# Block 1's keys, queries and output gates by seven products of block sums, and two of four forward state products in other PSUM banks

## The chip, the cores and the metric

The kernel runs on one core of one Trainium2 chip. The metric is the device time of one execution in microseconds (us). Five engines work side by side, each on its own queue in order: PE (TensorE, matrix products into PSUM), DVE (VectorE), ACT (ScalarE), POOL (GpSimd) and SP (SyncE, which only issues DMAs here). PSUM has eight banks; one 128x512 float32 tile fills one.

## The reference, cut to what matters

```
h = x + mlstm_mixer(rmsnorm(x), ...)          # S = 2048 tokens, D = 1024
  u = xn @ w_in                               # q, k: 512 columns each; v, o: 1024 each; 16 gates
  h_fwd = mlstm_scan(q, k, v, i, f); h_bwd = the same on the flipped sequence
     # per chunk of 128 tokens: num = (s*d) v + inter * q C;  C = decay*C + (w*v) k^T
  h = norm(h_fwd + h_bwd) * head_norm * sigmoid(o);  mix = h @ w_out
h = h + sqrelu_mlp(rmsnorm(h), w1, w2)        # D_FF = 4096
h = h + sigmoid(rmsnorm(h) @ gate_w + b) * (p @ ple_w);  out = rmsnorm(h)
```

The change touches the first product, `xn @ w_in`, for the upper half of the tokens, and the update of the forward state `C`.

## The kernel before

Every float32 product is three products of rounded parts: an operand is cut into a high part (cast to fp32r on ACT) and the rest (subtraction on DVE) by `split`, and `mm3` (L161) adds high*high, high*rest and rest*high in PSUM.

The tokens are two blocks of 1024. Block 1 comes first: its values and gates (tiles `psv`, two jobs of `v_jobs`), then 4 slabs of 128 key features, 4 of queries and 8 of output gates. A slab is a `slab_job`: for each 512 tokens `feat_group` runs 8 blocks of the contraction times 3 matmuls of 128x128 by 128x512 into one bank (`psf`), and ACT or DVE moves the result to an `ev` tile, which goes to DRAM (`kq_d`, `og_d`; keys also transposed to `kt_d`). `run` walks over the jobs: the weights of the next are split while the groups of the present one run. Steps woven in between prepare block 0's tokens (`Early`: load `raw`, squares on ACT into `junk`, scaling and 32x32 transposes on DVE, store to `mix_d`).

Block 0 follows in the same way, with the backward scan woven in; then the forward scan over 16 chunks. In a chunk PE does, in this order (table `ORDER`): `n0`, the forward numerators (4 tiles `pn`, one for each head); `s`, the state update (4 tiles `pu`, L100 by `state_update`, moved out on DVE as `Cn`); `T`, eight transposes into two tiles `pth`; `S`, the scores of the next chunk (`pS`); `n1`, the backward numerators (4 `pn`); `o0 o1`, the output product (2 `pso`). ACT moves `pn` out as `nt`.

PSUM is dealt out by tag: `ps_mm` has four banks (`pn`, `pso`, `psf`, `psv`, and before the change all forward `pu`), `ps_tr` has three (`pth`, `ptg`, `pt`), `ps_s` one (`pS`). A new tile of a tag takes a bank whose last tile has been read; PE waits for that. SBUF tiles are dealt out likewise: tag `H` has 39 slots of 4 KB a partition, `O` 7, `S` 6.

The MLP after the scan already works by seven products: a product of 2x2 blocks is made of 7 products of sums of blocks in place of 8 (`SEVEN`, `products`, `Left` for the weights' sums, `Job7`, `run7`). The seven accumulate in three banks; each bank is read out between its products, and the parts are added on DVE. Nearly all instructions are recorded on a helper's line, L100, so tiles tell them apart.

Of the kernel before, what the change touches and what calls it, by code (L numbers as in the profile page):

```python
# [16 lines left out]
P = 128  # L17
# [18 lines left out]
def hybrid_mlstm_kernel(  # L36
# [153 lines left out]
    class Weight:  # L190
# [3 lines left out]
            self.srcs = src if isinstance(src, list) else [src]  # L194
            self.shape = shape

        def dma(self):
            self.st = Ht("wst", self.shape)
# [158 lines left out]
    class Early(Prep):  # L357
# [20 lines left out]
                self.raw = None  # L378

        def get(self, m):  # L380
            self.z[m] = shuffled(self.d, m)

        def tr(self, k):
            t = Ht("xT", [P, 2, 512], F32R)
# [17 lines left out]
    wcol = const.tile([P, P], F32, name="wcol")  # L402
    ecol = const.tile([P, P], F32, name="ecol")
    dcb = const.tile([P, P], F32, name="dcb")


    gt = {}
# [14 lines left out]
    def store(c, dst, src):  # L422
        (SP if c >= 8 else G).dma_start(dst, src)
# [237 lines left out]
    def bwd_steps(c):  # L661
        s = {}

        def load():
            s["kt"] = kt_load(c, Ot)
            s["v"] = v_load(c)

        def one():
            s["vx"] = v_split(s["v"], m=V)
            s["wk"] = wk_of(s["kt"], 1, c)  # L670

        def two():
# [5 lines left out]
        return [load, one, two]  # L678


    wo = [rows_w(w_out, k * P) for k in range(KD)]
# [1 line left out]
    class Chunk:  # L683
# [130 lines left out]
        def out(self, n):  # L814
# [5 lines left out]
            if n == 1:  # L820
# [1 line left out]

    NF = DFF // P
    NQ = S // 256
    SEVEN = [("A11", "B11", 0), ("A12", "B21", 2), ("S2", "T2", 0), ("S1", "T1", 1), ("S3", "T3", 0),
             ("S4", "B22", 1), ("A22", "T4", 0)]  # L830
    sub_, add_ = ALU.subtract, ALU.add
# [7 lines left out]
    def products(A_, B_, n, after):  # L839
        ps = [None] * 3  # L840

        def product(i, an, bn, bk):
            def f():
                first = ps[bk] is None
                if first:
                    ps[bk] = (ps_mm, ps_mm, ps_tr)[bk]("p" + "abc"[bk])
                for k in range(n):
                    ah, al = A_.get(an, k)
                    bh, bl = B_.get(bn, k)
                    mm3(ps[bk], ah, al, bh, bl, first and k == 0, k == n - 1, skip_group_check=not first)  # L850
                after(i, ps[bk])
            return f
        return [product(i, *s) for i, s in enumerate(SEVEN)]

    def hi_lo(shape):

        n = 1
        for s in shape[1:]:
            n *= s
        if n <= 512:  # L860
            t = Ht("op", [P, 2] + list(shape[1:]), F32R)
            return t[:, 0], t[:, 1]
        return Ht("op", shape, F32R), Ht("op", shape, F32R)

    class Left:


        def __init__(self, n):
            self.n, self.ops = n, {}

        def preps(self, eng, eng2=None):
            n, eng2 = self.n, eng2 or eng

            def alloc():
                if n > 2:
                    self.s = [Ht("sa", [P, 2, n, P]) for _ in range(2)]
                else:
                    t = Ht("sa", [P, 4, n, P])
                    self.s = [t[:, 0:2], t[:, 2:4]]

            def s12():
                alloc()
                (r1, r2), s = self.r, self.s[0]
                eng.tensor_tensor(s[:, 0], r1[:, :, P:], r2[:, :, P:], op=add_)  # L884
                eng.tensor_tensor(s[:, 1], s[:, 0], r1[:, :, :P], op=sub_)

            def s34():
                (r1, r2), s = self.r, self.s
                eng2.tensor_tensor(s[1][:, 0], r1[:, :, :P], r1[:, :, P:], op=sub_)
                eng2.tensor_tensor(s[1][:, 1], r2[:, :, :P], s[0][:, 1], op=sub_)  # L890

            def op(names, src, cut):
                def f():
                    t = src()
                    hl = hi_lo(t.shape)
                    split(hl[0], hl[1], t)
                    for i, nm in enumerate(names):
                        self.ops[nm] = lambda k, i=i: tuple(cut(x, i, k) for x in hl)
                return f
            by_col = lambda x, i, k: x[:, k, i * P:(i + 1) * P]  # L900
            by_row = lambda x, i, k: x[:, i, k]
            return [s12, op(["A11"], lambda: self.r[0][:, :, :P], by_col),
                    op(["A12", "A22"], lambda: self.r[1], by_col), s34,
                    op(["S1", "S2"], lambda: self.s[0], by_row),
                    op(["S3", "S4"], lambda: self.s[1], by_row)]

        def get(self, nm, k):
            return self.ops[nm](k)

    class Left1(Left):  # L910


        def __init__(self, f):
            super().__init__(4)
            self.f = f

        def dma(self):
            self.r = []
            for j in range(2):
                t = Ot("wst", [P, 4, 256])  # L920
                SP.dma_start(t, w1[j * 512:j * 512 + 512, self.f * 256:self.f * 256 + 256].rearrange("(k p) n -> p k n", p=P))
                self.r.append(t)

    class Left2(Left):

# [58 lines left out]

        def get(self, nm, k):
            return self.pairs[k].ops[nm]

    class Right1:


        def __init__(self):
            self.z, self.ops = {}, {}

        def split(self, nm):
            for m in range(2):
                hl = hi_lo([P, 2, 512])
                split(hl[0], hl[1], self.z[nm, m])
                self.ops[nm, m] = hl

        def get(self, nm, k):  # L1000
            hi, lo = self.ops[nm, k // 2]
            return hi[:, k % 2], lo[:, k % 2]

    class Tokens0(Right1):

# [99 lines left out]
    class Job7:  # L1105
        def __init__(self, left, B_, n, after, prep=None):
            self.left, self.groups = left, products(left, B_, n, after)
            self.prep = left.preps(V) if prep is None else prep
            self.side, self.post = [], [[] for _ in self.groups]

    def run7(jobs):
        def dma(i):
            if i < len(jobs):
                jobs[i].left.dma()
        for i, j in enumerate(jobs):
            if i == 0:
                dma(1)
            dma(i + 2)
            nxt = jobs[i + 1].prep if i + 1 < len(jobs) else []

            def both(g, post):
                def f():
                    g()
                    for h in post:
                        h()
                return f
            weave([both(g, p_) for g, p_ in zip(j.groups, j.post)], nxt + j.side)

    def up_job(blk, B_, f):

# [156 lines left out]
    seq = []  # L1287
    for b in (1, 0):
        jobs[b, "v"] = v_jobs(pa[b], b)
        jobs[b, "k"] = [slab_job(pa[b], b, KC + h * P, kq_evac(0, h)) for h in range(H)]  # L1290
        jobs[b, "q"] = [slab_job(pa[b], b, QC + h * P, kq_evac(1, h), (ps_mm, (ps_tr, ps_mm)[b])) for h in range(H)]
        jobs[b, "o"] = [slab_job(pa[b], b, OC + j * P, o_evac(j)) for j in range(KD)]
# [46 lines left out]
    p0.tr1(3)  # L1339
    strict()  # L1340
    v0.groups = [lambda: weave(v0g[3:4], pa[1][1].steps()[2:])] + v0g[4:]
    jobs[1, "k"][0].side.append(lambda: gate_rows(1))
    jobs[1, "k"][1].side.append(gate_bias)

    for nm, pr in (("k", pa[0][0]), ("q", pa[0][1])):
        e = pr.early()
        for j, f in zip(jobs[1, nm], (e[0:1], e[1:2], e[2:4], e[4:6])):
            j.side += f
    o = jobs[1, "o"]
    o[5].side += pa[0][0].gets()  # L1350
    o[6].groups, o[7].groups = [o[6].groups[0], o[7].groups[0]], [o[6].groups[1], o[7].groups[1]]
    o[6].weights, o[7].weights = o[6].weights + o[7].weights, []
    o[7].side += pa[0][0].trs() + pa[0][1].gets()
# [196 lines left out]
```

## Time and profile before

| | |
|---|---|
| median of 3 runs | 2457.06 us (2454.72 to 2457.98) |
| profiled execution: time / span of its trace | 2456.72 / 2455.0 us |
| busy in the span: PE, DVE, ACT, POOL | 98%, 62%, 46%, 24% |
| block 1's keys, queries, gates | 117.9 to 296.1 us |
| forward scan, about | 604 to 957 us |

A busy matrix engine is no proof that it works at its peak: consecutive matmuls overlap in the profile, so the time that one costs is the distance between starts. The chunks and stages are told apart by the times at which their tiles appear.

### The profile page before, as it was taken

How to read it: one execution, taken by the hardware profiler on the slowest of the kernel's cores; microseconds unless marked ns; L12 is line 12 of the kernel's file. 1: busy time of each engine (PE TensorE's matmuls, PEld its weight loads, DVE VectorE, ACT ScalarE, POOL GpSimd, SP SyncE). 2: the span in 40 equal slices, each digit the busy share in tenths (PEclk: the TensorE clock that was granted, in tenths of full speed). 3: DMA queues.
4: the chain of work that ended last, by engine and by line, in shares of the span. 5: the costliest groups of instructions: out<-in, count | busy, mean ns of one | idle time of the engine just before them, and what ended most of it. 6: DMA issues, size and time to landing. Idle time of an engine off the chain costs nothing.

```text
span 2455.0 us, 31650 instructions
## 1 busy us (share of the span) xinstructions
PE 2402.5 (98%) x11413; PEld 1978.5 (81%) x11413; DVE 1514.4 (62%) x2533; ACT 1131.9 (46%) x2134; POOL 592.5 (24%) x609
## 2 busy tenths in 40 slices
PE   7999999999999999999999999999999999999998
PEld 6988898788888887888888888787887888887776
DVE  6152426556778888666674455766676667666665
ACT  5031414336777875343353333444443444445554
POOL 1030022124333333345633333011111111110000
PEclk9999999999999999999999999999999999999999
DMA  7178337868667775455763332567677776893211
GB/s 254 49 199 248 94 90 237 264 209 311 221 218 263 254 263 173 123 165 163 267 230 105 104 107 73 164 141 180 147 176 171 173 171 156 184 227 100 78 55 49
DMA packets 270133, 420.72 MB, mean 171 GB/s; under 512 B 46440, under 2 KB 181992, under 8 KB 269976
## 3 DMA queue, kind: packets, MB, share of 16 engines
q1 hardware_dynamic: 211416, 299.03, 37.3%
q0 software_dynamic: 58272, 119.15, 20.5%
q8 instruction: 89, 1.46, 0.2%
q14 instruction: 68, 0.56, 0.1%
q10 hardware_dynamic: 288, 0.52, 0.1%
HBM read 253.43 MB, written 165.01 MB: 170 GB/s over the span
## 4 chain that ended last, share of the span: by engine, by line
PE 54%; DVE 3%; ACT 1%; DMA 1%; issue 1%; SPq 0%; POOL 0%; ACTq 0%; DVEq 0%; POOLq 0%
PE pa L100 27%; PE pb L100 13%; PE pc L100 7%; PE pg L100 5%; PE pl L100 1%; DMA hst<-hid_d 1%; PE pt L100 1%; DVE h L100 1%; ACT L100 1%; DMA wst<-in_mlp_w 1%; DVE xs L100 1%; DVE op L100 1%; DVE rst L100 0%; DVE raw L100 0%; DVE g L100 0%
## 5 line engine op out<-in xcount | busy, mean ns | idle before, releaser
L100 PE MATMUL pa<-op 128*128 128x512 f32 x3072 | 754.2, 395 | 7.4 <-ACT e L100 4.3
L100 PEld LDWEIGHTS pa<-op 128*128 128x128 f32 x3072 | 575.4, 188 | 147.5 <-ACT e L100 7.2
L100 PE MATMUL pb<-op 128*128 128x512 f32 x1536 | 384.3, 394 | 0.9 <-DVE op L100 0.8
L100 PEld LDWEIGHTS pb<-op 128*128 128x128 f32 x1536 | 288.2, 188 | 70.0 <-DVE op L100 1.1
L100 PE MATMUL psf<-xT,whi 128*128 128x512 f32 x1024 | 322.0, 395 | 0.0
L100 DVE TENSOR_TENSOR op<-sa,op 128x768 fp32r<-128x768 f32 (+2 forms) x160 | 168.3, 1058 | 139.7 <-ACT op L100 106.8
L1162 POOL DMA_DIRECT2D h_d<-o x96 | 93.0, 976 | 563.3 <-DVE o L100 515.2
L100 PEld LDWEIGHTS psf<-xT,whi 128*128 128x128 f32 x1024 | 192.1, 189 | 43.9
L100 ACT COPY e<-pa 128x512 f32<-128x512 f32 x160 | 93.8, 586 | 259.4 <-PE pa L100 258.7
L100 ACT CAST op<-sa 128x768 fp32r<-128x768 f32 (+2 forms) x160 | 139.5, 879 | 147.8 <-PE pb L100 69.0
L100 PE MATMUL psf<-xT,wlo 128*128 128x512 f32 x512 | 202.2, 395 | 0.0
L100 PE MATMUL pc<-op 128*128 128x512 f32 x768 | 191.5, 394 | 0.2 <-DVE op L100 0.2
L100 PEld LDWEIGHTS pc<-op 128*128 128x128 f32 x768 | 144.1, 188 | 34.1 <-DVE op L100 0.6
L100 PE MATMUL psv<-whi,xT 128*128 128x272 f32 (+2 forms) x720 | 161.6, 318 | 0.6 <-DVE xT L98 0.6
L100 PEld LDWEIGHTS psv<-whi,xT 128*128 128x128 f32 x720 | 119.1, 189 | 9.9 <-DVE xT L98 0.8
L100 DVE TENSOR_TENSOR op<-wst,op 128x512 fp32r<-128x512 f32 x96 | 108.1, 1128 | 28.7 <-ACT op L100 16.1
L100 ACT CAST op<-wst 128x512 fp32r<-128x512 f32 x96 | 79.1, 834 | 95.1 <-DVE op L100 61.4
L884 POOL TENSOR_TENSOR sa<-wst 128x512 f32<-128x512 f32 x32 | 57.7, 1803 | 261.7 <-PE pb L100 158.2
L100 PEld LDWEIGHTS psf<-xT,wlo 128*128 128x128 f32 x512 | 96.6, 189 | 22.6
L100 PE MATMUL psv<-wlo,xT 128*128 128x272 f32 (+2 forms) x360 | 114.3, 317 | 0.0
L100 DVE TENSOR_TENSOR wlo<-wst,whi 128x1024 fp32r<-128x1024 f32 (+2 forms) x64 | 77.0, 1212 | 56.7 <-ACT whi L100 44.1
L100 PE MATMUL pso<-whi,hThi 128*128 128x512 f32 x256 | 102.4, 401 | 5.9 <-ACT nt L100 4.4
(228 smaller groups left out, 4257.5 us busy)
## 6 DMA issues: line engine op xcount, KB each, us to landing
wst<-in_mlp_w SPq DMA_DIRECT2D x96, 512.0 KB
h_d<-o POOLq DMA_DIRECT2D x96, 512.0 KB, 12.5
hid_d<-e SPq DMA_DIRECT2D x128, 256.0 KB
hst<-hid_d SPq DMA_DIRECT2D x64, 384.0 KB
wst<-in_mlstm_w_in SPq DMA_DIRECT2D x44, 512.0 KB
vst<-v_d SPq DMA_DIRECT2D x31, 512.0 KB
raw<-in_x SPq DMA_DIRECT2D x16, 512.0 KB
kq<-kq_d SPq DMA_DIRECT2D x16, 512.0 KB
```

The source lines that it names most:

```text
L100: r = f(*a, **kw)
L884: eng.tensor_tensor(s[:, 0], r1[:, :, P:], r2[:, :, P:], op=add_)
L1162: G.dma_start(rows(h1_d, 2 * q + i), o[i], accum_op=add_)
```

## The change

Two things. First, block 1's 16 slabs become 8 pairs of slabs. Of a pair the weights (1024x256) are 2x2 blocks of 512x128 and block 1's tokens (1024 features x 1024 tokens) 2x2 blocks of 512x512; the pair is made by the seven products, each of 4 blocks of the contraction times 3 matmuls. The sums of tokens `T1` to `T4` are made once on DVE while the values' second job runs, stored to DRAM (`ta_d`, by POOL's queue) and loaded again. The sums of weights are made for each pair on DVE. The transposed keys are stored by head pairs, in runs of 64 floats where there were 128. Second, in the forward scan the state products of heads 0 and 1 take `ps_tr` banks.

`products`, `hi_lo`, `Left`, `Right1`, `Job7` and `run7` are moved up in the file unchanged; `LeftW` is the old `Left1` for any weight and column. Steps that were hung on the slabs are hung on the pairs.

```diff
-            pu = (ps_tr if d == 1 and h % 2 else ps_mm)("pu")[:, :DVX]
+            pu = (ps_tr if (h % 2 if d == 1 else h < 2) else ps_mm)("pu")[:, :DVX]
...
+    class TokensA(Right1):
+        def parts(self, nm, k):
+            pr, k = self.prs[int(nm[2]) - 1], k + 4 * (int(nm[1]) - 1)
+            return pr.hi[k], pr.lo[k]
+        def get(self, nm, k):
+            return self.parts(nm, k) if nm[0] == "B" else super().get(nm, k)
...
+            return [t1, less("T2", "B22", "T1"), less("T3", "T2", "B11"), less("T4", "B21", "T2")]
...
+    def pair_job(B_, blk, col, finish, scale=None):
+        e = {}
+        def after(i, ps):
+            t = St("ev", [P, 512])
+            if i in (0, 2, 3, 6):
+                if scale is None:
+                    A.copy(t, ps)
+                else:
+                    A.activation(t, ps, AF.Copy, scale=scale)
+                if i < 6:
+                    e[i] = t
+                else:
+                    finish(t, 1, 0)
+            else:
+                t = e.pop({1: 0, 4: 3, 5: 2}[i])
+                if scale is None:
+                    V.tensor_tensor(t, ps, t, op=add_)
+                else:
+                    V.scalar_tensor_tensor(t, ps, scale, t, op0=ALU.mult, op1=add_)
+                finish(t, *{1: (0, 0), 4: (1, 1), 5: (0, 1)}[i])
+        left = LeftW(w_in, col)
+        return Job7(left, B_, 4, after)
...
-    seq = [j for nm in "vkqo" for j in jobs[1, nm]]
-    seq += [jobs[0, "v"][1], jobs[0, "v"][0]] + jobs[0, "k"] + o[:6] + [qa, fin]
+    pairs1 = kp + qp + op_
+    seq = [jobs[0, "v"][1], jobs[0, "v"][0]] + jobs[0, "k"] + o[:6] + [qa, fin]
...
+    for n, pr in ((0, pa[0][0]), (2, pa[0][1])):
         e = pr.early()
+        pairs1[n].side += e[0:2]
+        pairs1[n + 1].side += e[2:6]
...
+    mk = [xa.make(m) for m in range(2)]
+    vj.side += [f for i in range(4) for f in (mk[0][i], mk[1][i])]
+    vj.side += [f1.left.dma, lambda: xa.zload("T2"), lambda: xa.zload("T1")] + f1.prep[:3] + [lambda: xa.split("T2")] + f1.prep[3:] + [
+        lambda: xa.split("T1")]
+    f1.post[0] += [lambda: xa.zload("T3"), lambda: xa.zload("T4")]
...
+    run([v0, vj])
+    run7(pairs1)
+    jobs[0, "v"][1].ready = True
     run(seq)
```

PE's queue where the values of block 1 end and the keys begin. Before, the gates' transpose `ptg` and then the slabs:

```order
L100 MATMUL psv<-wlo,xT 128x256
L100 MATMUL psv<-whi,xT 128x256
L100 MATMUL ptg<-ident,gt 128x128
L100 MATMUL psf<-xT,whi 128x512 x2
L100 MATMUL psf<-xT,wlo 128x512
```

Now:

```order
L100 MATMUL psv<-wlo,xT 128x256
L100 MATMUL psv<-whi,xT 128x256
L100 MATMUL pa<-xT,op 128x512 x12
L100 MATMUL pc<-xT,op 128x512 x12
L100 MATMUL pa<-op 128x512 x12
L100 MATMUL pb<-op 128x512 x12
L100 MATMUL ptg<-ident,gt 128x128
L100 MATMUL pa<-op 128x512 x12
L100 MATMUL pb<-xT,op 128x512 x12
L100 MATMUL pa<-op 128x512 x12
```

The seven products of a pair stand one after the other, and `ptg` has moved behind the fourth.

ACT's queue from the fourth product of the first pair to the first of the second, now (`z` are the loaded token sums, `sa` the weights' sums, `op` the high and low parts, `junk` the squares of block 0's tokens):

```order
L100 ACTIVATE ev<-pb 128x512
L100 CAST op<-z 128x1024
L100 CAST op<-sa 128x1024 x2
L100 ACTIVATE junk,sse_1361<-raw 128x1024
L100 ACTIVATE ev<-pa 128x512
L100 ACTIVATE junk,sse_1361<-raw 128x1024 x2
L100 CAST op<-wst 128x512
L100 ACTIVATE junk,sse_1361<-raw 128x1024
L100 ACTIVATE ev<-pa 128x512
```

Casts and squares stand between two readings of a product's bank, where before they stood between readings of finished slabs.

PE's queue in a chunk of the forward scan (chunk 8) from the last state product on. Before:

```order
L100 MATMUL pu<-vh,wk 128x258
L100 MATMUL pth<-ident,jk 128x128 x8
L100 MATMUL pS<-kq 128x128 x4
L100 MATMUL pn<-vh,pTh 128x258
L100 MATMUL pn<-vl,pTh 128x258
```

Now:

```order
L100 MATMUL pu<-vh,wk 128x258
L100 MATMUL pth<-ident,jk 128x128 x4
L100 MATMUL pS<-kq 128x128
L100 MATMUL pth<-ident,jk 128x128 x4
L100 MATMUL pS<-kq 128x128 x3
L100 MATMUL pn<-vh,pTh 128x258
```

The second `pth` has moved behind a score product here and in chunks 1, 2 and 9; in the other chunks the order of PE is as it was. The orders of DVE and ACT in the scan are unchanged but for one step in chunk 1.

## Rows read from the trace of the kernel before

**Rows 1.** The page: busy times, the granted clock by slices, a costly group.

```profile
PE 2402.5 (98%) x11413; PEld 1978.5 (81%) x11413; DVE 1514.4 (62%) x2533; ACT 1131.9 (46%) x2134; POOL 592.5 (24%) x609
...
PEclk9999999999999999999999999999999999999999
...
L100 PE MATMUL psf<-xT,whi 128*128 128x512 f32 x1024 | 322.0, 395 | 0.0
```

**Rows 2.** Busy times by stretch: length, each engine, granted clock, DMA share, GB/s.

```profile
60.00:118.00 58.00, 58.00 (x435) 55.85 (x433) 6.35 (x18) 3.79 (x9) 0.00 (x0) 1.00 0.14 48
118.00:296.00 178.00, 178.00 (x770) 144.19 (x769) 66.47 (x121) 51.51 (x77) 28.18 (x48) 1.00 0.62 185
604.00:720.00 116.00, 110.14 (x660) 95.70 (x660) 90.38 (x183) 88.23 (x243) 44.53 (x56) 1.00 0.71 240
720.00:957.00 237.00, 227.46 (x1329) 197.67 (x1327) 205.41 (x393) 183.92 (x486) 76.35 (x89) 1.00 0.72 245
957.00:1340.00 383.00, 380.94 (x1637) 306.92 (x1638) 249.90 (x268) 152.15 (x216) 183.10 (x129) 1.00 0.54 173
```

**Rows 3.** Waits of PE, 604 to 940: us in total, times, longest.

```profile
PE pn L100 <- DVE Cn L100: 4.7, 6, 1.6
PE pso L100 <- ACT nt L100: 4.4, 6, 1.4
PE pu L100 <- ACT nt L100: 2.5, 6, 0.8
```

**Rows 4.** PE's timeline at both ends of block 1's slabs: start, length.

```profile
117.95 0.71 PE L100 MATMUL psf<-xT,whi 128*128 128x512 f32 x2
...
295.90 0.39 PE L100 MATMUL psf<-xT,wlo 128*128 128x512 f32 x1
296.13 0.28 PE L100 MATMUL psv<-whi,xT 128*128 128x272 f32 x1
```

**Rows 5.** Groups by shape on DVE and ACT in the MLP's stages: busy, mean ns.

```profile
L100 DVE TENSOR_TENSOR op<-wst,op 128x1024 fp32r<-128x1024 f32 x3 | 3.7, 1219 | 0.9 <-PE pa L100 0.9
...
L100 DVE TENSOR_TENSOR e<-pc,e 128x512 f32<-128x512 f32 x3 | 2.0, 683 | 1.6 <-PE pc L100 1.6
...
L100 ACT CAST op<-sa 128x1024 fp32r<-128x1024 f32 x31 | 32.5, 1050 | 58.5 <-PE pb L100 30.0 <-DVE op L100 14.8 <-issue 6.4
L100 ACT COPY e<-pa 128x512 f32<-128x512 f32 x30 | 17.5, 583 | 61.9 <-PE pa L100 61.9
```

**Rows 6.** Waits of PE in the MLP's first product, 957 to 1340.

```profile
PE pa L100 <- ACT e L100: 1.5, 1, 1.5
PE pa L100 <- DVE op L100: 0.7, 1, 0.7
PE pa L100 <- DVE e L100: 0.4, 2, 0.2
```

**Rows 7.** DMA issues: KB each, median us from issue to landing.

```profile
kt_d<-y POOLq DMA_DIRECT2D x16, 128.0 KB, 5.8
```

**Rows 8.** PE's timeline in chunk 13, and DVE's reading of the state products.

```profile
872.28 1.03 PE L100 MATMUL pth<-ident,jk 128*128 128x128 f32 x8
873.15 1.06 PE L100 MATMUL pS<-kq 128*128 128x128 f32 x8
873.97 0.36 PE L100 MATMUL pn<-vh,pTh 128*128 128x258 f32 x1
...
873.03 1.66 DVE L100 SCALAR_TENSOR_TENSOR Cn<-Cn,dcb,pu 128x258 f32<-128x258 f32 x4
```

**Rows 9.** The same in chunk 14, up to the output product.

```profile
893.61 1.03 PE L100 MATMUL pth<-ident,jk 128*128 128x128 f32 x8
896.65 0.39 PE L100 MATMUL pn<-vh,pTh 128*128 128x258 f32 x1 [1.11 <-DVE Cn L100]
...
901.18 0.51 PE L100 MATMUL pso<-whi,hThi 128*128 128x512 f32 x1 [0.49 <-ACT nt L100]
...
896.12 1.65 DVE L100 SCALAR_TENSOR_TENSOR Cn<-Cn,dcb,pu 128x258 f32<-128x258 f32 x4
```

More of the change, by code (lines that the diff above doesn't have):

```diff
@@ L404, in hybrid_mlstm_kernel, with products, product, f @@
     dcb = const.tile([P, P], F32, name="dcb")
+    NF = DFF // P
+    NQ = S // 256
+    SEVEN = [("A11", "B11", 0), ("A12", "B21", 2), ("S2", "T2", 0), ("S1", "T1", 1), ("S3", "T3", 0),
+             ("S4", "B22", 1), ("A22", "T4", 0)]
+    sub_, add_ = ALU.subtract, ALU.add
+    def products(A_, B_, n, after):
+        ps = [None] * 3
+        def product(i, an, bn, bk):
+            def f():
+                first = ps[bk] is None
+                if first:
+                    ps[bk] = (ps_mm, ps_mm, ps_tr)[bk]("p" + "abc"[bk])
+                for k in range(n):
+                    ah, al = A_.get(an, k)
+                    bh, bl = B_.get(bn, k)
+                    mm3(ps[bk], ah, al, bh, bl, first and k == 0, k == n - 1, skip_group_check=not first)
+                after(i, ps[bk])
+            return f
+        return [product(i, *s) for i, s in enumerate(SEVEN)]
@@ new lines, in hybrid_mlstm_kernel, with __init__, dma, split @@
+    class LeftW(Left):
+        def __init__(self, w, c0):
+            super().__init__(4)
+            self.w, self.c0 = w, c0
+        def dma(self):
+            self.r = []
+            for j in range(2):
+                t = Ot("wst", [P, 4, 256])
+                SP.dma_start(t, self.w[j * 512:j * 512 + 512, self.c0:self.c0 + 256].rearrange("(k p) n -> p k n", p=P))
+                self.r.append(t)
+    class Right1:
+        def __init__(self):
+            self.z, self.ops = {}, {}
+        def split(self, nm):
+            for m in range(2):
+                hl = hi_lo([P, 2, 512])
+                split(hl[0], hl[1], self.z[nm, m])
+                self.ops[nm, m] = hl
+        def get(self, nm, k):
+            hi, lo = self.ops[nm, k // 2]
+            return hi[:, k % 2], lo[:, k % 2]
@@ new lines, in hybrid_mlstm_kernel, with __init__, run7, dma @@
+    class Job7:
+        def __init__(self, left, B_, n, after, prep=None):
+            self.left, self.groups = left, products(left, B_, n, after)
+            self.prep = left.preps(V) if prep is None else prep
+            self.side, self.post = [], [[] for _ in self.groups]
+    def run7(jobs):
+        def dma(i):
+            if i < len(jobs):
+                jobs[i].left.dma()
+        for i, j in enumerate(jobs):
+            if i == 0:
+                dma(1)
+            dma(i + 2)
+            nxt = jobs[i + 1].prep if i + 1 < len(jobs) else []
+            def both(g, post):
+                def f():
+                    g()
+                    for h in post:
+                        h()
+                return f
+            weave([both(g, p_) for g, p_ in zip(j.groups, j.post)], nxt + j.side)
@@ L678, in bwd_steps, with __init__, get, make @@
         return [load, one, two]
+    ta_d = dram.tile([4, 2, P, 2, 512], F32, name="ta_d")
+    class TokensA(Right1):
+        def __init__(self, prs):
+            super().__init__()
+            self.prs = prs
+        def parts(self, nm, k):
+            pr, k = self.prs[int(nm[2]) - 1], k + 4 * (int(nm[1]) - 1)
+            return pr.hi[k], pr.lo[k]
+        def get(self, nm, k):
+            return self.parts(nm, k) if nm[0] == "B" else super().get(nm, k)
+        def make(self, m):
+            s = {}
+            def new(nm):
+                s[nm] = Ot("z", [P, 2, 512])
+            def store(nm):
+                G.dma_start(ta_d[int(nm[1]) - 1, m], s[nm])
+            def t1():
+                new("T1")
+                for i in range(2):
+                    t, (h2, l2), (h1, l1) = s["T1"][:, i], self.parts("B12", 2 * m + i), self.parts("B11", 2 * m + i)
+                    d = St("d", [P, 512])
+                    V.tensor_tensor(t, h2.bitcast(F32), h1.bitcast(F32), op=sub_)
+                    V.tensor_tensor(d, l2.bitcast(F32), l1.bitcast(F32), op=sub_)
+                    V.tensor_tensor(t, t, d, op=add_)
+                store("T1")
+            def less(nm, a, b):
+                def f():
+                    new(nm)
+                    for i in range(2):
+                        t = s[nm][:, i]
+                        if a[0] == "T":
+                            for n_, x_ in enumerate(self.parts(b, 2 * m + i)):
+                                V.tensor_tensor(t, s[a][:, i] if n_ == 0 else t, x_.bitcast(F32), op=sub_)
+                        else:
+                            h_, l_ = self.parts(a, 2 * m + i)
+                            V.tensor_tensor(t, h_.bitcast(F32), s[b][:, i], op=sub_)
+                            V.tensor_tensor(t, t, l_.bitcast(F32), op=add_)
+                    store(nm)
+                return f
+            return [t1, less("T2", "B22", "T1"), less("T3", "T2", "B11"), less("T4", "B21", "T2")]
+        def zload(self, nm):
+            for m in range(2):
+                self.z[nm, m] = Ot("z", [P, 2, 512])
+                SP.dma_start(self.z[nm, m], ta_d[int(nm[1]) - 1, m])
@@ new lines, in kq_pair, with finish @@
+    def kq_pair(B_, blk, qk, hp):
+        yy = {}
+        def finish(t, i, l):
+            h, c0 = 2 * hp + i, blk * 8 + 4 * l
+            t = t.rearrange("p (c t) -> p c t", c=4)
+            SP.dma_start(kq_d[c0:c0 + 4, :, qk, h, :].rearrange("c p t -> p c t"), t)
+            if qk:
+                return
+            if l not in yy:
+                yy[l] = [Ht("y", [P, 2, 8, 2, 32]), 0]
+            y = yy[l][0]
+            for m in range(2):
+                V.transpose(y[:, m, :, i, :], t[:, 2 * m:2 * m + 2].rearrange("p c (b i) -> p (c b) i", i=32))
+            yy[l][1] += 1
+            if yy[l][1] == 2:
+                for m in range(2):
+                    for a in range(4):
+                        G.dma_start(kt_d[(c0 + 2 * m) * P:(c0 + 2 * m + 2) * P, a, 64 * hp:64 * hp + 64].rearrange("(b i) e -> i b e", i=32),
+                                    y[32 * a:32 * a + 32, m].rearrange("i b h j -> i b (h j)"))
+        return pair_job(B_, blk, (QC if qk else KC) + hp * 256, finish, None if qk else DK ** -0.5)
@@ L681, in hybrid_mlstm_kernel, with o_pair, finish @@
+    def o_pair(B_, blk, jp):
+        def finish(t, i, l):
+            j, c0 = 2 * jp + i, blk * 8 + 4 * l
+            act(t, t, AF.Sigmoid)
+            V.tensor_scalar_mul(t, t, gains["hn"][:, j:j + 1])
+            SP.dma_start(og_d[c0:c0 + 4, :, j, :].rearrange("c p t -> p c t"), t.rearrange("p (c t) -> p c t", c=4))
+        return pair_job(B_, blk, OC + jp * 256, finish)
     wo = [rows_w(w_out, k * P) for k in range(KD)]
@@ L837, in hybrid_mlstm_kernel @@
     tz_d = dram.tile([4, 2, P, 2, 512], F32, name="tz_d")
[L839 to L908, printed above, removed]
@@ L910, in hybrid_mlstm_kernel @@
-    class Left1(Left):
-        def __init__(self, f):
[L914 to L922, printed above, removed]
+    class Left1(LeftW):
+        def __init__(self, f):
+            super().__init__(w1, f * 256)
@@ L986, in get @@
             return self.pairs[k].ops[nm]
[L988 to L1002, printed above, removed]
     class Tokens0(Right1):
@@ L1103, in zload @@
                     SP.dma_start(self.z[nm, m], tz_d[int(nm[1]) - 1, m])
[L1105 to L1127, printed above, removed]
     def up_job(blk, B_, f):
```

84 lines of the change are left out of this document (66 added, 18 removed).

## The prediction

> **What bounds the kernel now.** I read the page's busy times first, then stretches, then PE's waits. PE is busy 98% of the span at the upper of its two clock levels (2.4 GHz) nearly throughout [rows 1], so only two things can shorten the kernel: fewer or shorter matmuls, and less of the little time in which PE waits. The stretches say where that is. Block 1's slabs, 118 to 296 us, have PE busy 178 of 178 us, with DVE at 66 and ACT at 52 [rows 2]: there every matmul taken away is worth its full price, and DVE and ACT have room. The forward scan is another matter: from 604 to 957 PE is idle for 15 us while DVE is at 78 and 87% [rows 2], and PE's waits are for PSUM banks that DVE (`Cn`) or ACT (`nt`) has not yet read [rows 3].
>
> **The price of a matmul.** The group row gives 395 ns for one 128x512 matmul [rows 1], but that is from entry to end, and they overlap. The first of block 1's slab matmuls starts at 117.95, and the first one behind them at 296.13 [rows 4]. In between are 16 slabs x 2 halves x 8 x 3 = 768, so one costs 178.18 / 768 = 0.232 us. This is the price that I use; 0.395 would overstate the change by 70%. The Trainium skill, TensorE: Matmul & The Clock Gate, section Back-to-back issue gap, gives about 131 ns for matmuls of 512 columns in a sustained stream with their weight loads. By it the change would save 96 x 0.131 = 12.6 us; this stage itself shows 232, so the measurement decides and the figure gets no chance.
>
> **Removed.** A pair of slabs cost 96 matmuls, and costs 7 x 4 x 3 = 84 now. 8 pairs: 96 fewer, 96 x 0.232 = **22.3 us less**, at the same shapes and the same clock. The stage should take 672 x 0.232 = 155.9 us.
>
> **Added: the token sums.** T1 is made in 12 operations of 128x512 on DVE, T2 to T4 in 8 each, 36 in all. At 0.683 us (a 128x512 addition, rows 5) that is 24.6 us. With them come the first pair's 4 weight sums (2.7 us), its low parts (3.5 tiles of 1024 at 1.219, 4.3 us) and the low parts of T2 and T1 (4.9 us): 36.5 us of DVE. They stand beside the values' matmuls, 60 to 118 us, in which DVE works for 6 of 58 us [rows 2]. So they are hidden and I take nothing; without that cover they would cost all of 36.5. The DMAs that carry the sums out and back (8 MB) fall where the DMA engines are busy 14% of the time [rows 2]. T3 and T4 are fetched only in the first pair, but are wanted by its fifth and seventh product, 11.1 and 16.7 us after its start.
>
> **Added: read-outs between products.** A product is 12 matmuls, 2.78 us, a pair 84, 19.5 us. Its first, third, fifth and last product add into one bank, so ACT or DVE must have read that bank while the one product in between runs: 0.58 us of work (ACT's copy, rows 5) under a cover of 2.78. What can be late is the queue: casts of 1.05 us [rows 5], or the squares of block 0's tokens, stand before the read-out. In one pair DVE now does 4 sums, 3.5 low parts and 3 additions, 2.7 + 4.3 + 2.0 = 9.1 us; if all it did before in this stage stays (66 us / 8 = 8.3, an upper bound, since old splits and copies are in it) it is at 17.4 of 19.5. ACT does 3.5 casts and 4 copies, 6.0, at most 6.4 more from before: 12.4 of 19.5. Both fit, DVE without much to spare. A wait is below nothing in no case, since PE had none here. The nearest row is the MLP's first product, the same seven products: 383 us hold 2.6 us of such waits, 2.2 of them where the stage is entered [rows 6]. This stage has an entry too, so I take **2.4 us**; for the range 0 to 12 (the starved pairs below).
>
> **The two moved state products.** They were put where PE waits most: for the first `pn` of `n1` until DVE has read `pu` (4.7 us in 6 chunks), and for `pu` until ACT has read `pn` (2.5 us) [rows 3]. With heads 0 and 1 in `ps_tr` both waits lose their cause. But `ps_tr` has three banks: two `pu` and the first `pth` fill them, so the second `pth` must wait until DVE has read a `pu`. That wait is the old one in an earlier place. What it is worth stands in two chunks:
> - Chunk 13, no wait before: `pth` starts at 872.28, its second half 0.43 later at 872.71, scores at 873.15, `pn` at 873.97 [rows 8]. DVE starts on `Cn` at 873.03; chunk 14 shows PE going on 0.53 us after that start (896.12, 896.65) [rows 9]. The second `pth` could start at 873.56, so PE loses 0.85 us.
> - Chunk 14, a wait of 1.11 before: the second `pth` starts when `pn` did, at 896.65, and only then come its 0.44 us and the scores' 0.82, which used to run under the wait. `pn` is 1.26 later. Behind it `pso` waited 0.49 for ACT [rows 9], whose order hangs on DVE and not on PE, so that much is absorbed: 0.77 lost.
>
> I went through all chunks in the same way. 7 and 10 are like 13 (0.6, 0.5); 8, 11 and 12 like 14 (0.5, 0.7, 0.8; in 8 three of the four scores still come behind); in 9 the loss of 0.6 goes into a `pso` wait of 1.0; chunk 2 gains the 0.6 that `pu` waited for `nt`; in 1 and 4 what is gained goes into the next wait; in 3, 5 and 6 DVE is in time. Sum: 0.85 + 0.77 + 1.1 + 2.0 - 0.6 = **4.1 us more**. Its bounds are -7.2 (both waits vanish and nothing takes their place) and +10 (eight chunks at 1.26).
>
> **The sum.** The profiled execution took 2456.72 us (span 2455.0), 0.3 under the median of 2457.06. 2456.7 - 22.3 + 2.4 + 4.1 = **2441 us**.
>
> **Rivals.**
> - *The banks do help.* If DVE came to `Cn` before the second `pth` in chunks 7 to 14, as it does in 3, 5 and 6, the waits of 7.2 us would go, part of it into `pso`; I take 5. For it: DVE follows PE in some chunks, so that an earlier `pu` could pull `Cn` forward. Against it: in chunk 14 DVE starts `Cn` 2.5 us after `pth` began. 2456.7 - 22.3 + 2.4 - 5 = 2432 us.
> - *Starved pairs.* The low parts and token sums now hold 28 of 39 `H` slots (12 tiles of block 1's tokens, 16 of sums), and 11 are left for a pair's 7, the next pair's 9, and the transposes `y`. A `y` slot comes free when its DMA has landed, 5.8 us after issue for 128 KB [rows 7]. The key stores are now twice as many with runs of 256 bytes. If in four early pairs an operand waits for such a slot, PE loses 5.8 less a cover of 2.78, 12 us in all in place of 2.4: 2450.5 us. For it: POOL's queue carries both kinds of `y` in the first four pairs. Against it: products five and six need their operands late in a pair. The Trainium skill, DMA: Bandwidth & Descriptors, section Specifications, says that transfers under 512 bytes miss the line rate, as the DMA engine then reads, changes and writes back. That speaks against these stores; no row here shows runs of 256 bytes.
> - *Slower than before.* ACT reads the pairs' first bank late in every pair. The gain of 22.3 less 4.1 is used up at 18.2 / 8 = 2.3 us of waits in each pair. That needs read-outs that come 2.78 + 2.3 = 5.1 us after a product, five casts in a row before one copy. ACT's order has at most three casts or squares there. At 4 us a pair it would be 2456.7 - 22.3 + 4.1 + 32 = 2470 us.
> - *The price is another.* If the sevenfold products ran at another spacing than 0.232 the saving would scale; PE's clock is full in both stages [rows 2], and nothing speaks for it.
>
> **Chances.** Forecast 66%, with a range of its own of 2436 to 2447; banks help 17%; starved pairs 13%; slower 3%; another price 1%. The range of 2431 to 2450 holds the forecast, the case of the banks, and the milder half of the starved pairs. A measurement of this kernel can tell about 0.2%, 5 us, from no change. Faster by more than that (under 2452): 94%, the forecast, the banks and most of the starved pairs. Within it 4%, slower 2%.
>
> **What would show it.** Right: 672 matmuls `pa`, `pb`, `pc` in some 156 to 159 us; DVE near 40 us between 60 and 118, PE busy throughout; waits of PE in the pairs of 1 to 4 us, most in the first two; in the scan a new wait `pth <- DVE Cn` in chunks 7 to 14, `pn <- Cn` gone, `pso <- nt` smaller, and PE's idle time there larger than before. Wrong: the scan shorter (the banks help); waits of PE for `op` in pairs 1 to 4 with DVE waiting for a DMA of `kt_d` or `mix_d` (starved); waits of `pa` for ACT's `ev` in every pair (slower).

## The result and the profile after

The changed kernel takes **2441.27 us** (median of 4 runs, 2440.1 to 2444.73), the kernel before 2455.94 beside it (4 runs, 2454.72 to 2457.98). The ratio is 0.9942, 95% interval 0.9925 to 0.9959: 10 to 18 us faster. The forecast was 2441. The profiled execution took 2440.1 us with a span of 2438.4, 16.6 less than the span before.

The page of the changed kernel: busy time, granted clock by slices, the group that answers to `psf` [rows 1].

```profile
PE 2379.7 (98%) x11317; PEld 1962.4 (80%) x11317; DVE 1592.3 (65%) x2641; ACT 1168.6 (48%) x2182; POOL 606.3 (25%) x633
...
PEclk9999999999999999999999999999999999999999
...
L100 PE MATMUL pa<-op 128*128 128x512 f32 x3360 | 824.7, 394 | 7.7 <-ACT e L100 4.0
```

96 matmuls are gone (11413 to 11317); the mean of this group is 394 ns, that of `psf` was 395. The stretches that answer to [rows 2] (length, PE, PEld, DVE, ACT, POOL, granted clock, DMA share, GB/s):

```profile
60.00:116.00 56.00, 56.00 (x426) 54.20 (x425) 38.13 (x65) 12.03 (x18) 4.53 (x8) 1.00 0.66 228
116.00:273.00 157.00, 156.44 (x675) 126.22 (x675) 105.35 (x175) 73.72 (x111) 37.74 (x64) 1.00 0.71 215
579.00:695.00 116.00, 109.73 (x665) 96.50 (x664) 90.79 (x183) 88.82 (x244) 44.19 (x56) 0.99 0.71 241
695.00:941.00 246.00, 231.35 (x1322) 202.33 (x1320) 204.67 (x391) 186.22 (x485) 76.40 (x89) 0.97 0.69 236
941.00:1324.00 383.00, 380.75 (x1637) 307.18 (x1638) 252.36 (x269) 152.64 (x216) 182.67 (x129) 1.00 0.54 173
```

Three things are to be seen. DVE works 38 us ahead of the pairs, where it worked 6, and PE doesn't notice. The pairs keep PE busy for 156.4 of 157 us. And the scan's second stretch is 9 us longer than before, at a granted clock of 0.97 instead of 1.00. PE's timeline at both ends of the pairs, which answers to [rows 4] (start, length):

```profile
115.94 1.32 PE L100 MATMUL pa<-xT,op 128*128 128x512 f32 x5
...
270.11 2.96 PE L100 MATMUL pa<-op 128*128 128x512 f32 x12
272.92 0.29 PE L100 MATMUL psv<-whi,xT 128*128 128x272 f32 x1
```

From 115.94 to 272.92 are 156.98 us for 672 matmuls, against 178.18 for 768: **21.2 us less**. PE's waits in the changed kernel (us in total, times, longest), which answer to [rows 3]:

```profile
PE pth L100 <- DVE Cn L100: 14.6, 11, 3.0
...
PE pso L100 <- ACT nt L100: 3.5, 5, 2.0
...
PE pu L100 <- ACT nt L100: 0.7, 1, 0.7
...
PE pa L100 <- ACT ev L100: 0.6, 1, 0.6
```

The wait `pn <- Cn` is gone and `pth <- Cn` stands in its place, three times as large. The wait for `ev` is the only one in the pairs. Cutting both timelines at the same instructions (the stage's first product; the `psv` behind it; the `pu` of chunk 0; the MLP's first `pa`; the end of the span) shows where the 16.6 us come from:

| stretch | before | after | difference |
|---|---|---|---|
| up to block 1's keys | 117.95 | 115.94 | -2.0 |
| block 1's keys, queries, gates | 178.2 | 157.0 | -21.2 |
| up to the scan | 289.8 | 287.8 | -2.0 |
| scan, chunk 0's `pu` to the MLP | 343.2 | 352.6 | **+9.4** |
| MLP to the end | 1525.9 | 1525.0 | -0.9 |

The total agrees with the forecast, but not by the forecast's terms: the scan lost 9.4 us where 4.1 were expected, and 4.0 us came from two stretches in which no matmul was taken away.

**The granted clock.** Falls of the clock that happened in one execution and not in the other are more than enough for those 4.0 us. Between 462 and 474 us the kernel before had a granted clock of 0.72 (3.4 us lost), the changed one at the same place (438 to 450) 1.00. Between 36 and 48 us the window of the kernel before shows 0.86:

```profile
36.00:48.00 12.00, 10.46 (x48) 8.18 (x48) 7.69 (x14) 5.11 (x9) 0.00 (x0) 0.86 0.73 246
```

The same window of the changed kernel shows 1.00:

```profile
36.00:48.00 12.00, 10.46 (x59) 8.41 (x59) 11.47 (x20) 7.48 (x13) 0.00 (x0) 1.00 0.23 68
```

And that of the changed kernel run again shows 0.86:

```profile
36.00:48.00 12.00, 10.46 (x53) 8.47 (x53) 10.07 (x17) 6.18 (x10) 0.00 (x0) 0.86 0.23 67
```

0.14 of 12 us is 1.7 us, the price of one fall by the clock. In the scan the changed kernel had five. What PE lost by one can be read in chunk 7, which has a fall in the changed kernel and none in the same kernel run again: PE is busy 22.7 us in the one and 21.2 in the other. Chunk 12 shows how a fall comes. The timelines of PE, DVE and POOL in the changed kernel (start, length, waits in brackets; `rsy` and `xs` belong to the norm of the MLP's tokens, `rd` are the divisors of the numerators, `ib` is the next chunk's queries times a loaded factor, `mb` the decay weights of the scores):

```profile
831.19 0.60 PE L100 MATMUL pth<-ident,jk 128*128 128x128 f32 x4
834.82 0.84 PE L100 MATMUL pth<-ident,jk 128*128 128x128 f32 x4 [3.03 <-DVE Cn L100]
835.45 1.91 PE L100 MATMUL pS<-kq 128*128 128x128 f32 x8
...
829.23 0.16 DVE L100 TENSOR_TENSOR rsy<-rsy,rst 128x1 f32<-128x1 f32 x1
829.42 2.28 DVE L100 SCALAR_TENSOR_TENSOR xs<-raw,rsy,row_mlp 128x1024 f32<-128x1024 f32 x1
831.63 2.55 DVE L100 SCALAR_TENSOR_TENSOR rd<-nt 128x4 f32<-128x4 f32 x1
834.21 0.17 DVE L100 TENSOR_TENSOR rd<-rd,ecol 128x4 f32<-128x4 f32 x1
834.29 1.66 DVE L100 SCALAR_TENSOR_TENSOR Cn<-Cn,dcb,pu 128x258 f32<-128x258 f32 x4
...
829.33 1.29 POOL L976 TENSOR_TENSOR ib<-kq,ib 128x512 f32<-128x512 f32 x1 [11.86 <-PE pn L100]
831.69 1.23 POOL L986 TENSOR_SCALAR_AFFINE_SELECT mb<-mb 128x512 f32<-128x512 f32 x2
832.88 1.26 POOL L976 TENSOR_TENSOR ib<-kq,ib 128x512 f32<-128x512 f32 x1
```

The windows around it in the same kernel:

```profile
824.00:830.00 6.00, 6.00 (x40) 5.43 (x39) 3.85 (x12) 5.02 (x17) 0.67 (x1) 1.00 0.76 291
830.00:836.00 6.00, 2.97 (x23) 2.73 (x22) 5.97 (x8) 1.96 (x8) 4.13 (x6) 0.93 1.02 352
836.00:842.00 6.00, 6.00 (x41) 5.92 (x41) 4.30 (x9) 5.12 (x10) 2.69 (x4) 0.78 0.01 3
842.00:848.00 6.00, 6.00 (x27) 4.88 (x26) 5.20 (x12) 5.24 (x16) 0.00 (x0) 1.00 0.79 233
```

Read the timelines from their end. The second `pth` starts 0.53 us behind `Cn`, as the forecast had it. `Cn` is late because DVE still has the norm of the MLP's tokens (`xs`) and `rd` ahead of it, and these take 2.28 and 2.55 us: `rd` runs beside three operations of POOL (two `mb`, one `ib`) and ends at 834.18, just as `ib` does (834.14), while its neighbour of the same size takes 0.17. PE waits 3.03 us, and then works on at the lower level of 1.2 GHz for a while: the eight `pS` take 1.91 us, where chunk 13 of before took 1.06 [rows 8]. The windows lose 0.07 and 0.22 of 6 us each, 1.7 us again.

### The profile page after: what moved, and what is told of

Read it like the earlier page. It is cut to its first block, busy times and chain, and to the rows that moved or that the text cites. A ratio compares the mean times of both kernels' runs of the same rounds, so it can differ in the third digit from the quotient of the medians.

```text
span 2438.4 us, 31719 instructions
## 1 busy us (share of the span) xinstructions
PE 2379.7 (98%) x11317; PEld 1962.4 (80%) x11317; DVE 1592.3 (65%) x2641; ACT 1168.6 (48%) x2182; POOL 606.3 (25%) x633
## 4 chain that ended last, share of the span: by engine, by line
PE 54%; DVE 4%; DMA 2%; ACT 2%; issue 1%; SPq 0%; POOL 0%; ACTq 0%; DVEq 0%; POOLq 0%
PE pa L100 28%; PE pb L100 14%; PE pc L100 7%; PE pg L100 4%; DMA hst<-hid_d 1%; PE pl L100 1%; ACT L100 1%; DVE h L100 1%; DVE xs L100 1%; PE pt L100 1%; DMA wst<-in_ple_w 1%; DVE op L100 1%; DVE rst L100 0%; DVE raw L100 0%; ACT g L100 0%
## 5 line engine op out<-in xcount | busy, mean ns | idle before, releaser
L100 PE MATMUL pa<-op 128*128 128x512 f32 x3360 | 824.7, 394 | 7.7 <-ACT e L100 4.0
L100 PEld LDWEIGHTS pa<-op 128*128 128x128 f32 x3360 | 629.6, 188 | 160.0 <-ACT e L100 6.9
L100 PE MATMUL pb<-op 128*128 128x512 f32 x1632 | 407.5, 394 | 0.9 <-DVE op L100 0.8
L100 DVE TENSOR_TENSOR op<-sa,op 128x1024 fp32r<-128x1024 f32 (+2 forms) x176 | 187.5, 1071 | 149.1 <-ACT op L100 113.9
L100 ACT CAST op<-sa 128x1024 fp32r<-128x1024 f32 (+2 forms) x176 | 156.3, 894 | 171.5 <-PE pb L100 84.3
L100 PE MATMUL psf<-xT,whi 128*128 128x512 f32 x512 | 160.6, 394 | 0.0
L100 PEld LDWEIGHTS psf<-xT,whi 128*128 128x128 f32 x512 | 95.2, 188 | 21.4
L100 PE MATMUL pg<-whi,xTl 128*128 128x512 f32 x256 | 101.9, 398 | 0.0
L100 PE MATMUL pso<-wlo,hThi 128*128 128x512 f32 x256 | 101.4, 397 | 0.0
L100 PE MATMUL pso<-whi,hTlo 128*128 128x512 f32 x256 | 101.2, 396 | 0.0
```

Source lines behind the costliest of these rows:

```text
L100: r = f(*a, **kw)
```

## Experiments

The median of the kernel before lay between 2454.9 and 2456.9 in the sets below, so ratios are the better comparison. "Waits" are the sum of `pth <- Cn`, `pn <- Cn`, `pso <- nt` and `pu <- nt`; "scan" runs from chunk 0's `pu` to the MLP, and "falls" are those of the granted clock in it. Stage, waits, scan and falls are from the one profile of each kernel.

| kernel | median, us | ratio to before, 95% | stage | waits | scan | falls |
|---|---|---|---|---|---|---|
| before | 2454.9 to 2456.9 | 1 | 178.2 | 11.6 | 343.2 | 0 |
| changed | 2441.27 | 0.9925 to 0.9959 | 157.0 | 18.8 | 352.6 | 5 |
| changed, again | 2441.8 | 0.9934 to 0.9959 | 156.1 | 18.1 | 350.1 | 4 |
| pairs only | 2439.14 | 0.9919 to 0.9947 | 156.2 | 16.2 | 350.4 | 1 |
| banks only | 2456.65 | 0.9995 to 1.0013 | 178.2 | 14.1 | 342.2 | 1 |
| head 0 only | 2437.09 | 0.9919 to 0.9942 | 156.6 | 14.0 | 343.9 | 0 |
| heads 2 and 3 | 2440.38 | 0.9923 to 0.9949 | 156.4 | 16.5 | 348.1 | 2 |
| scores first | 2438.32 | 0.9918 to 0.9945 | 156.3 | 14.7 | 347.1 | 2 |
| token sums twice | 2436.29 | 0.9910 to 0.9938 | 156.1 | 17.0 | 345.8 | 2 |
| head 0, scores first | **2435.01** | 0.9904 to 0.9932 | 156.3 | 17.8 | 346.3 | 0 |
| store from POOL | 2437.6 | 0.9901 to 0.9933 | 156.5 | 14.0 | 342.8 | 0 |

### The parts alone

Pairs only:

```diff
-            pu = (ps_tr if (h % 2 if d == 1 else h < 2) else ps_mm)("pu")[:, :DVX]
+            pu = (ps_tr if d == 1 and h % 2 else ps_mm)("pu")[:, :DVX]
```

> The changed kernel with the bank choice of the forward state products put back; only the pairs are left of the change. Theory: the pairs alone bring about 24 us (stage 157 us instead of 178, and 2 to 3 us ahead of it), and the two moved state products lose about 9.5 us, because the second pth waits for DVE's Cn and the granted clock falls after the waits of 2 us. Then this kernel takes 2441.3 - 9.5 = about 2432 us, the waits pth<-Cn are gone, pn<-Cn is back at about 4.7 us, and windows of 6 us in the scan show no granted clock under 0.99. Rival, the banks cost the 4.1 us of the forecast and the rest is in other stages: 2437. Rival, the banks cost nothing or help: 2441 or more.

Banks only: the kernel before with the first of these two lines.

> The kernel before with the bank choice alone. Theory: slower by about 9.5 us, 2465, with waits pth<-Cn of about 15 us in all and falls of the granted clock behind the longest of them, as in the changed kernel. Rival, 4.1 us as forecast: 2460. Rival, the scan's loss comes from the pairs (their pools or their timing), not from the banks: 2456, and no pth<-Cn wait.

Both theories of the scan fell. The banks alone cost 1.7 us by the medians (interval -1.2 to +3.2): less than the 4.1 of the forecast, and nothing like 9.5. The last rival has this time, but not its missing wait (below). On top of the pairs the banks cost 2.1 to 2.7 by the medians and 2.2 to 3.4 by the ratios; the two kernels were timed in different sets and their intervals overlap, so that this can be told neither from nothing nor from 4.1. The pairs alone bring 16.4 us by the ratio (13.0 to 19.9), 5.6 less than their own stage gives. The scan of this kernel has the same instructions in the same order on every engine as before, and is 7.2 us longer in its profile: 5.4 more of PE's idle time, and one fall of 1.7. Waits of PE with the pairs alone:

```profile
PE pn L100 <- DVE Cn L100: 7.3, 7, 2.0
PE pso L100 <- ACT nt L100: 5.3, 8, 1.4
PE pu L100 <- ACT nt L100: 3.6, 6, 1.3
```

They are the waits of [rows 3], each larger: 16.2 us in place of 11.6. With the banks alone:

```profile
PE pth L100 <- DVE Cn L100: 10.0, 10, 2.1
...
PE pso L100 <- ACT nt L100: 3.5, 5, 2.0
...
PE pu L100 <- ACT nt L100: 0.6, 1, 0.6
```

So the exchange that the forecast described is there in both programs: `pn <- Cn` and most of `pu <- nt` go, `pth <- Cn` comes, 2.5 us more without the pairs and 2.6 with them. The pairs add 4.6 or 4.7 in either.

### Other heads

`h < 1` and `h > 1` in place of `h < 2`.

> The changed kernel with head 0 alone in ps_tr. Theory, the loss comes from the count of three banks: one pu and two pth fill them, no pth waits for Cn, the granted clock does not fall in the scan, and about 2430 us, within 2 us of the kernel with the pairs alone, or up to 4 us under it, if head 0's place in ps_tr shortens the waits pn<-Cn. Rival, any state product in ps_tr makes a transpose wait: 2436 to 2441.

> The changed kernel with heads 2 and 3 in ps_tr in place of heads 0 and 1. Theory: the second pth now waits for the Cn of head 2, two Cn later on DVE (1.0 us), in nearly every chunk: waits pth<-Cn over 22 us, more falls of the granted clock, 2450 to 2458 us. Rival, it does not matter which two heads lie there: 2441.

With head 0 only, no `pth` waits: one `pu` and two `pth` fill three banks. That part of the theory holds, and so does the distance: the time is 2.1 us under that of the pairs alone. It is 2437 and not 2430 because the pairs alone are 7 us above what was expected of them. Beside the waits with the pairs alone, the wait moves one step on:

```profile
PE pso L100 <- ACT nt L100: 10.7, 13, 1.7
...
PE pn L100 <- DVE Cn L100: 2.4, 4, 1.3
```

Heads 2 and 3 missed by 10 us. In the timeline of this kernel the eight `pS` (in chunk 10), or these and two `pn` (in chunk 8), run ahead of the second `pth`, so that part of the longer wait is filled: the edit changed the order too, and is no clean test of which heads lie there.

### The same kernel again, and the scores first

The changed kernel without an edit, and with its chunks in another order (ORDER_1 and ORDER_X alike):

```diff
-    ORDER = "n0 d1 s e T S p1 q n1 d2 k w sl m v d o0 o1 me".split()
+    ORDER = "n0 d1 s e S T p1 q n1 d2 k w sl m v d o0 o1 me".split()
```

> The changed kernel once more, nothing edited. Theory, the falls of the granted clock in the scan and the DVE operations that last 1.2 us beside POOL's come by the execution, while the waits pth<-Cn belong to the kernel: pth<-Cn again 10 to 15 us in about ten chunks, the pairs again 156 to 157 us, but the number of falls in the scan between one and six, each 1.7 us, and the scan without them within 3 us of 344. Median 2440 to 2442. Rival, falls belong to the kernel: the same five places again.

> The changed kernel with the scores ahead of the transposes in chunks 1 to 14, so that 0.8 us of other matmuls run while the second pth waits for DVE's Cn. Theory, the wait is for Cn and longer waits bring the falls: pth<-Cn shrinks from 10 to 15 us to under 5, no wait of 2 us and no fall of the granted clock in the scan, 2441.3 - 5 to - 9 = 2432 to 2436 us. Rival, the time goes to the next wait, since DVE is the one that sets the chunk's length: pn<-Cn or pso<-nt grow by as much, and 2440 to 2443.

Run again, the kernel shows the same: `pth <- Cn` 14.0 us in 11 waits, and falls behind four of the five waits that had them before (the fifth wait was 0.7 us long this time, in place of 2.0). So the waits belong to the kernel, and the falls mostly follow the waits. Over the eleven profiles of the table the scan has 26 of PE's waits between 1.85 and 3.03 us, and 17 of them are followed by a fall; of nine waits between 1.40 and 1.71 us none is. With the scores first `pth <- Cn` falls to 8.3, `pso <- nt` grows from 3.4 to 5.5, and the median is 3.5 us under that of the changed kernel in the same set, where 5 to 9 were expected; the intervals overlap. Two of these waits, of 1.9 and 2.7 us, still have a fall behind them, where no fall was expected.

### The cover of the token sums

T1 and T2 are each made twice:

```diff
-                for i in range(2):
+                for i in [0, 1, 0, 1]:
...
-                    for i in range(2):
+                    for i in ([0, 1, 0, 1] if nm == "T2" else [0, 1]):
```

> The changed kernel with the token sums T1 and T2 made twice: 20 more DVE operations of 128x512, 13.7 us, ahead of the pairs, where DVE has about 18 us free. Theory, the token sums lie beside the values' matmuls: within 2 us of the changed kernel, and DVE 13 us busier between 60 and 116 us. Rival, the cover is thin and the first pairs wait for T2's or T1's low parts: 5 to 14 us more, with waits pa<-op or pc<-op in the first pair.

Hidden but for 1.0 us. The stretch ahead of the pairs and the pairs, in this kernel:

```profile
60.00:119.00 59.00, 57.99 (x433) 55.66 (x432) 47.62 (x83) 12.55 (x19) 4.52 (x8) 1.00 0.55 192
119.00:275.00 156.00, 156.00 (x674) 126.09 (x673) 107.30 (x178) 73.94 (x111) 37.96 (x64) 1.00 0.74 225
```

DVE is at 47.6 us in place of 38.1, and the stage takes 156.1. Ahead of it PE now waits once, 1.0 us, for DVE to read the gates (`psv <- gt`), which it does not in the changed kernel: the cover of the forecast's sums holds, but not much more would fit under it. That the median is 5 us under that of the changed kernel in the same set was expected by no theory. The edit doesn't touch the scan, which had two falls instead of four or five; such distances between kernels are as large as what the banks do.

### Head 0 and scores first

Both edits together.

> Head 0 alone in ps_tr, and the scores ahead of the transposes. Theory: no pth waits, pn<-Cn of 2.4 us goes too since 0.8 us of scores no longer stand between the transposes and pn but the order of the heads is the same; 2434 to 2437 us, not above the kernel with head 0 alone. Rival, the transposes come 0.8 us later, the low parts hTlo with them, and pso waits for these: 2438 to 2441.

The lowest median, 2435.01: 17 to 24 us faster than before, and 6.8 under the changed kernel in the same set. The way there was not the expected one: `pn <- Cn` grew from 2.4 to 7.0 instead of going. What its profile shows is that the longest of these waits is 1.7 us and the scan has no fall: PE is idle for 19.7 us in it, as in the changed kernel (19.4), and the scan is 6.3 us shorter. As the lowest of nine medians it is also in part a matter of choice.

### Where the late Cn comes from

The token norm of chunk 12 above stands ahead of `Cn`. It was moved behind the transposes and scores of the next chunk, in the changed kernel, with the pairs only, and in the kernel before:

```diff
-    ORDER_X = "n0 d1 s e T S p1 q n1 xt d2 k xl w sl m v d o0 o1 me xn".split()
+    ORDER_X = "n0 d1 s e T S xn p1 q n1 xt d2 k xl w sl m v d o0 o1 me".split()
...
+            elif nm == "xn":
+                tp.get(c - 1, [lambda: None] * 3)[1]()
```

> The changed kernel with the norm of the MLP's tokens (step xn, 2 us of DVE work that ends a chunk and stands ahead of the next chunk's Cn) moved behind the transposes and scores. Theory: Cn is late in chunks 7 to 14 because this norm stands ahead of it on DVE, and 1.2 us more where its 128x1 operations run beside POOL's ib; without it the second pth waits under 4 us in all instead of 14, no fall of the granted clock from chunk 7 on, these chunks take 21.2 to 21.8 us each, and the kernel about 2430 us. Rival: DVE's total work sets the chunk, the wait comes back as pn<-Cn, pt<-xs or pso, and 2439 to 2442.

> The pairs without the two moved state products, with the norm moved in the same way. Theory: with Cn in time it no longer matters where the state products lie; within 3 us of the changed kernel with the norm moved, about 2430. Rival: the banks decide, and it stays at 2437 to 2440.

> The kernel before with the norm moved, nothing else. Theory: the scan's collisions took 3 to 6 us more with the pairs than without them; with the norm moved the scan takes the same in both, so this kernel is 20 to 23 us above the pairs with the norm moved, the 21 to 22 us that the pairs' own stage gives: 2450 to 2453. Rival: the pairs lengthen the scan by another way, and the distance stays at 16 to 18 us.

They took 2460.14, 2459.9 and 2479.07 us (before: 2455.07). Waits of PE in the first:

```profile
PE pso L100 <- ACT nt L100: 20.8, 12, 2.6
...
PE pt L100 <- DVE xs L100: 7.9, 17, 1.5
PE pth L100 <- DVE Cn L100: 3.3, 4, 1.1
```

The norm has a part in the late `Cn`: without it there `pth <- Cn` falls from 14.6 to 3.3. How large a part this does not show, since chunks 8 to 13 are also some 2 us longer here than in the changed kernel, which gives DVE more time. On the time both sides missed: the rival had the way, a wait at another place, but 2439 to 2442. ACT's square for the norm now stands ahead of the `nt` copies, `pso` waits 20.8 us for them, often with a fall behind, and all three kernels are 19 to 24 us slower. The distance between pairs and no pairs is 19.2 us here, between the two expectations. In the two profiles the stage differs by 22.0 us (178.2 and 156.2), and chunks 7 to 13 take 178.2 us with the pairs and 177.5 without. So where another chain sets the chunk, the pairs do not lengthen these chunks.

The last run takes POOL's `ib` away from the norm:

```diff
-                SP.dma_start(x0_d[t // 4, :, :, sl].rearrange("k p t -> p k t"), z)
+                G.dma_start(x0_d[t // 4, :, :, sl].rearrange("k p t -> p k t"), z)
```

> The changed kernel with the store of the MLP's transposed tokens (x0_d<-zt, chunks 7 to 14) issued from POOL's queue in place of SP's, where it waits 10 to 11 us for ACT and holds back the loads kq, mb and ib of the chunk after next. Theory: part of the scan's loss is DVE's 128x1 operations of the token norm that last 1.2 us beside POOL's ib, in the last 2 us of a chunk, ahead of Cn. With ib landing some 3 us earlier the two no longer meet: Cn begins 1.9 to 2.8 us after a chunk's first pu in place of 3.5 to 4.5, pth<-Cn falls from 14 us to 4 to 8, at most one fall of the granted clock behind such a wait, and 2430 to 2436 us. Rival: ib still ends beside the norm, or POOL, waiting for zt, is late with ib itself; the collisions stay or move to other small operations, and 2439 to 2443 us.

Half right. The first `ib` starts 16 to 19 us into chunks 7 to 13 in place of 20 to 24, and the norm's 128x1 operations meet it in chunk 8 alone; but the chain of `me` (the end of the norm over the heads), operations of 128x4, meets it in chunks 9 to 13, and `pth <- Cn` stays at 10.3. Its longest wait is now 1.8 us and the scan has no fall, though `pso` waits 2.0 us once, in chunk 1. Chunks 7 to 13 of the kernel before as one window:

```profile
736.30:892.20 155.90, 149.88 (x927) 132.68 (x926) 133.10 (x280) 128.03 (x358) 54.10 (x69) 1.00 0.77 264
```

Of the changed kernel:

```profile
710.50:877.10 166.60, 154.88 (x927) 138.26 (x926) 134.50 (x282) 131.22 (x358) 54.98 (x71) 0.96 0.72 247
```

And of this one:

```profile
714.10:870.80 156.70, 148.81 (x927) 132.06 (x925) 134.54 (x278) 127.24 (x356) 64.67 (x76) 1.00 0.77 262
```

The same 927 matmul records in each. PE's idle time is 6.0, 11.7 and 7.9 us, and the changed kernel's PE is busy 5 us longer for the same work, the lower clock. The median of 2437.6 is above the expected range.

## Why the prediction was right, and where it was not

- **The price of a matmul and the 22.3 us.** Right. All kernels with pairs have their stage in 156.1 to 157.0 us in the table, 21.2 to 22.1 less. The 131 ns that the prediction gives from the Trainium skill (TensorE: Matmul & The Clock Gate, section Back-to-back issue gap), and the saving of 12.6 us by it, are not borne out here: 672 matmuls in 156 us are 0.232 us each, as in [rows 4].
- **The token sums hidden.** Right: DVE at 38.1 us, "near 40", and 9.5 us more in that stretch cost 1.0.
- **The read-outs, 2.4 us.** Too dear. The wait for `ev` in the changed kernel is 0.6 us in all, one late read-out, and the stage is never more than 1.1 over 672 x 0.232 = 155.9 in the table (2.0 in the changed kernel with the norm moved). The waits of 1 to 4 us in the pairs that were to be a sign did not come. Nor did starved pairs; `kt_d`'s stores with runs of 256 bytes showed no wait of PE.
- **The two moved state products, 4.1 us.** The mechanism is right: `pth <- Cn` waits in each of chunks 7 to 14, `pn <- Cn` is gone, `pso <- nt` is a little smaller. But it waits in chunks 2, 4 and 6 as well (0.8, 0.7 and 0.7 us), where the working had a gain, no loss, and DVE in time. The size was taken from the timing of `Cn` before, as if it would stay; in chunk 12 `Cn` begins 4.5 us after the chunk's first `pu` in place of 3.2. Alone the banks cost 1.7 us by the medians, with the pairs 2.1 to 2.7, and neither can be told from nothing. The term had no place for the granted clock: behind the wait of 3.03 us another 1.7 are lost.
- **What no term had.** The sum takes the scan as unchanged but for the moved products, and that failed. With the pairs alone the scan is 7 us longer than before, in the same order of instructions, and the pairs bring 16.4 us instead of 19.9 (22.3 less 2.4). By these numbers some 4 to 6 us of the changed kernel's time belong to no term of the sum. The two terms that were too dear, by 1.8 and about 2 us, made up for most of them, so that the sum met 2441 to 0.3 us by luck. What the prediction had for good reasons is the saving of the pairs and the exchange of waits.
- **The rival that the banks help, 2432.** Wrong as a whole: with the banks undone the kernel is not slower.

What stays open: why the scan is longer with the pairs. Its instructions are those of before in the same order, so the difference lies in when they run. Shown is that `Cn` is late behind the token norm, that with the store from POOL, which moves `ib`, chunks 7 to 13 take 156.7 us, and that these chunks are equal with and without pairs once another chain sets them. The store was not moved in the kernel before, so it is not shown that this gives back what the pairs cost and not something that the kernel before would gain too. Nor is it shown that the pairs make DVE and POOL meet more often: over the scan DVE's operations exceed their usual lengths by some 46 us in the kernel before and in the changed one, and by 55 with the pairs only (each operation against the tenth percentile of its group, summed).

## What to carry to other kernels

- Price matmuls by start-to-start time in their own stage; that term held to 5% in each of the nine profiles with pairs in the table.
- A saving in a stage that PE fills came through whole in that stage; the risk is in the stages where PE waits for engines that are nearly full. There kernels with nearly the same program differed by several us, so a small edit there needs its own run beside a repeat of the kernel it is compared with.
- Where a wait of PE can't be avoided, ask how long it is, and not only what the waits add up to: the three kernels of the table whose longest wait in the scan is 1.6 or 1.7 us had no fall of the clock in it, and behind 17 of the 26 longer waits there was one. That short waits are cheaper at the same sum rests on one pair of profiles, the changed kernel and head 0 with the scores first.

## Unexpected of the hardware

- **DVE behind POOL.** A DVE operation of 128x4 took 2.55 us instead of 0.17 beside three of POOL's, and `xs` 2.28 instead of the 1.28 or 1.29 of four other chunks. The Trainium skill, SBUF — State Buffer, section Who interferes with whom, says that a DVE instruction with two inputs in SBUF contends with a POOL instruction that reads SBUF, for a port pair that is locked by one of them at a time; the ends at 834.18 and 834.14 agree.
- **The granted clock falls inside a busy stream.** After a wait of 3.03 us, which ended at 834.82, PE ran at the lower level in part of the time up to 842 us, at a cost of 1.7; other falls (36 to 48 us) came in one execution of the same program and not in another. By the clock each is 1.7 us of difference between two executions of one kernel.
